# A third kind of unit in the seven-product pairs: one k-tile pair split in halves, in two gate pairs and both projection pairs, and nine instead of eleven matmuls on a constant ahead of the first product

## The chip, the cores and the metric

The kernel runs on one core of a Trainium2 chip. TensorE (PE) multiplies into PSUM; VectorE (DVE), ScalarE (ACT) and GpSimd (POOL) work elementwise; SyncE (SP) issues most loads from HBM on its queue, and POOL's queue issues a few that accumulate. The metric is the device time of one execution in microseconds, the median of several. Before the change it is 1359.29 us (three runs, 1358.73 to 1360.31).

## What is computed

One encoder block over 256 tokens of width 2048, in float32:

```python
h = rms_norm(x, g_mix[layer])
proj = h @ w_in[layer]            # heads of mixers A, B, C, and three gates
...                               # dilated, grouped-query and memory attention: oa, ob, oc
gates = sigmoid(gt).reshape(b, s, N_BRANCH, D_MODEL)
merged = (gates[:, :, 0] * (oa @ w_br_a[layer]) + gates[:, :, 1] * (ob @ w_br_b[layer])
          + gates[:, :, 2] * (oc @ w_br_c[layer]))
x = x + merged @ w_o[layer]
hf = rms_norm(x, g_ffn[layer]) @ w_ffn_in[layer]
x = x + (silu(hf[..., :D_FF]) * hf[..., D_FF:]) @ w_ffn_out[layer]
```

The change touches the gates and the branch products (the merging pairs), the projection by `w_o`, and the first microseconds of the kernel.

## The kernel before

**Products.** A float32 product is three products of rounded operands: ACT writes `whi`, the weight rounded (L433), DVE writes `wlo`, the rest (`raw - whi`, L443), and PE multiplies hi by hi, hi by lo and lo by hi into one PSUM bank (L79). Activations are split once, into two tiles per k-tile pair. A weight block is 128 x 1024: two k-tiles of 512 columns, one load of 512 KB by SP into one of eleven buffers (seven `raw`, two `more`, two halves of `both`); there are five pairs of `whi` and `wlo`. A buffer is free for the next load when its last reader has run, mostly the `wlo` subtraction.

**Pairs.** `pair` computes two blocks of 512 columns (0 and 1) for two halves of the tokens, four PSUM banks. The 2048 rows of weights are eight units of two k-tiles. A *whole* unit of column block 0 or 1 (steps `d0` to `d7` and `D0` to `D7`) takes 12 matmuls of 512 columns. A *double* takes two units and both column blocks together, in seven products X, W, P, Y, Z, Q, H of 6 matmuls for each of its two k-tiles instead of eight (the Winograd form of Strassen's scheme): 42 matmuls per unit pair and column pair and 48 without. It needs sums of tokens (`forms`, made by `token_sums`, and again split into hi and lo) and sums of weights: the first by an accumulating load on POOL's queue, those of P (L576), Q (L578) and H (L580) on DVE, each a 128 x 1024 addition. When the last X, P and Q products of a pair are done, ACT and DVE move partial sums between the banks (L553 to L562).

**Order.** A list of steps stands for each pair: front, back and end. `l0`, `r0` load the four blocks of a double, a letter with a number is a product, and a dot in the front is a place where a step of the end of the pair before it is put. `run` goes through the steps of all pairs of a chain and calls each step's first part (loads, sums, hi on ACT, and lo on DVE one step later) four steps ahead of its matmuls. PE and SP keep this order; on ACT and DVE the splits keep theirs among themselves, and a scheduler sets the rest (evacuations, `sg`, `mg`, transposes) between them.

**Stages.** In the profiled run: keys and values of the memory tokens to 47 us, queries, keys, values and attention to 286, the gates and the product of the first branch for column blocks 0 and 1 to about 313, then five merging pairs (gates of two column blocks in `pair`, with the branch products as dots' fillers and sigmoids and merges at L883 to L903): pair 0 at 313 to 352, pair 1 to 402, pair 2 to 454, pair 3 to 511, pair 4 to 570. Pairs 1 and 2 are those of the second branch; each pair takes the units 0 to 3 as two doubles and 4 to 7 whole. Then two projection pairs by `w_o` (to 614 and 658; one double, six whole units; the residual is added at L947) with the transposes of the result into `x1T` beside them, and the FFN to the end.

**The start.** Eleven matmuls of a 128 x 128 constant, float32 and so two passes each, run into an unused bank (L345 and L346) until the first weights are there. The first unit of column block 0 is loaded and split by k-tile (2 x 128 x 512), that of block 1 whole.

Of the kernel before, what the change touches and what calls it, by code (L numbers as in the profile page):

```python
# [57 lines left out]
STEPS_O = ("l0 X0 . r0 W0 . P0 Y0 . Q0 .", "Z0 D2 H0 D3 d2 D6 d3 D7 D4 D5", "d6 d7 d4 d5")  # L58
STEPS_O2 = ("l0 X0 . r0 W0 . P0 Y0 . Q0 .", "Z0 D2 H0 D3 d2 D4 D5 d3 D6 D7", "d4 d5 d6 d7")
# [44 lines left out]
def encoder_block(ctx: ExitStack, tc: tile.TileContext, a: dict, out: bass.AP):  # L104
# [106 lines left out]

    def release(raw):

        free.append(place_of.pop(id(raw))[1])
# [83 lines left out]
    def transposed(src, dst, g=None, lag=1, also=None):  # L298
# [3 lines left out]
        for h in range(2):  # L302
            if h:
                yield lag
            tp = bank("tp", "tp")
            for k in range(2):
                for t in range(T):
                    nc.tensor.transpose(tp[:, k * S + t * P:k * S + (t + 1) * P],
                                        src[t][:, (2 * h + k) * P:(2 * h + k + 1) * P], ident)
            if g is None:  # L310
                d = dst(2 * h, 2)
                split(d[0], d[1], tp.rearrange("p (k s) -> p k s", s=S))
            else:
                for k in range(2):
                    d = dst(2 * h + k, 1)
                    split(d[0], d[1], tp[:, k * S:(k + 1) * S], g(2 * h + k))
            if also is not None:
                if full is None:
                    full = s4([P, 2, 4, P], "ffull")
                to, of = full[:, :, 2 * h:2 * h + 2], tp.rearrange("p (k t s) -> p k t s", t=T, s=P)  # L320
                if g is None:
                    nc.scalar.activation(to, of, AF.Copy)
                else:
                    for k in range(2):
                        nc.scalar.activation(to[:, k], of[:, k], AF.Copy, scale=g(2 * h + k))
        if also is not None:
            token_sums(full, also)

    def token_sums(full, to):


        raw = s4([P, 2, 4, P], "fraw")
# [12 lines left out]
    for _ in range(11):  # L345
# [74 lines left out]
    def halves(*srcs, each=None):  # L420
# [5 lines left out]
        n = 0  # L426
        for v in srcs:
            v = v.unsqueeze(1) if len(v.shape) == 2 else v
            o = slice(n, n + v.shape[1])
            if each:  # L430
                low(0)
                each(n)
            nc.follow(nc.scalar.activation(hi[:, o], v, AF.Copy))  # L433
            due.append((lo[:, o], v, hi[:, o].bitcast(F32)))
# [5 lines left out]
    def low(n):  # L440

        while len(due) > n:
            nc.follow(nc.vector.tensor_sub(*due.pop(0)))  # L443

    def pair(src, lhs, lists, done, doubles=(), forms=None, operand=None, fresh="", early=False, by_halves=False):
# [12 lines left out]
        left = {"Y": 2 * nd + 2 * wholes["d"], "X": 6 * nd, "V": 2 * nd + 2 * wholes["d"],  # L458
                "W": 4 * nd + 2 * wholes["D"], "Q": 2 * wholes["D"]}
# [3 lines left out]
        stops = {"X": [left["X"] - n * nd for n in (2, 4, 6)], "W": [left["W"] - 2 * nd]}  # L463
# [30 lines left out]
        def whole(u, c):  # L494
            def ready():
# [11 lines left out]
                hi, lo = halves(*(raw[:, k] for k in range(PK)) if parts == 2 else (raw,),  # L507
# [24 lines left out]
        def begin2(m):  # L532
            j = doubles[m][1]
            raws[m].update({"b22": load((src(j, 1),), 0, PK), "b21": load((src(j, 0),), 0, PK)})
# [6 lines left out]
        def phase_end(kind, hi):  # L541
            seen[kind] = seen.get(kind, 0) + 1
            if seen[kind] < nd:
# [19 lines left out]

        def seventh(kind, m):
            of = {"X": "b11", "W": "t", "Y": "b21", "P": "t", "Z": "b22", "Q": "b11", "H": "b21"}[kind]
            bk = {"P": "X", "Q": "X", "H": ends[0][1], "Z": "W"}.get(kind, kind)
            needs = {"Y": "X", "P": "X", "Z": "P", "Q": "P", "H": "Q"}

            def ready():
                r = raws[m]  # L570
                raw = r[of]
# [7 lines left out]
                elif kind == "H":  # L579
                    nc.follow(nc.vector.tensor_add(raw, r["t"], raw))  # L580
                hi, lo = halves(raw)
                for n in {"Q": ["b11"], "Z": ["b22"], "H": ["t", "b21"]}.get(kind, ()):
                    release(r.pop(n))

                def products():
                    assert kind not in needs or seen.get(needs[kind], 0) == nd, (kind, seen)
                    assert kind != "Z" or seen["W"] == nd
                    for i in range(2):
# [4 lines left out]
                        mul(bk, st, hi[:, i], lo[:, i])  # L593
# [5 lines left out]
        def step(o):  # L599
# [5 lines left out]
            if kind in "lr":  # L605
                return lambda: (begin if kind == "l" else begin2)(n)
# [262 lines left out]
    mT, x1T, x, room = {}, [], [], []  # L869
    ss1 = const.tile([P, T, 4], F32, name="ss1")  # L870
    by_room = lambda tiles: lambda m, i, f: (tiles()[m][:, i, 0, (f + 1) % 4], tiles()[m][:, i, 1, (f + 1) % 4])
    TWO = (0, 1), (2, 3)

    def merging():
        nth = 0
        for b, (g0, k0, k1) in enumerate(((0, 0, 2), (8, 2, 6), (4, 6, 12))):
            for j in (0, 2) if b else (2,):
# [16 lines left out]
                def merge(c, r, j, b, sg):  # L894
# [4 lines left out]
                    def later():  # L899
# [4 lines left out]
                        if b == 2:  # L904
                            to = mT[j + c] = s8([P, 2, 4, S], "mT", pool=home(j + c))
                            if j + c == 0:
                                room.extend(form_room(1))
                            yield 4
                            yield from transposed([mg[t][:, n0:n0 + NC] for t in range(T)],
                                                  lambda k, n: (to[:, 0, k:k + n], to[:, 1, k:k + n]),  # L910
                                                  lag=2, also=room[0] if j + c == 0 else None)
                    if b:
                        start(urgent(later()))

                front, back, end = pair(block_pair(a["w_gate"], g0 + j), xT, STEPS_GATE[min(nth, 2)], gates, TWO,
                                        by_room(lambda: gforms), early=nth == 0, fresh="Y" if nth < 2 else "")
# [9 lines left out]
    def projecting():  # L926
# [16 lines left out]
        for n in (0, 2):  # L943
# [22 lines left out]
            yield pair(block_pair(a["w_o"], n), mTl, STEPS_O2 if n else STEPS_O, add, TWO[:1], by_room(lambda: room))  # L966
# [139 lines left out]
```

## Time and profile before

| | |
|---|---|
| median of three runs | 1359.29 us |
| the profiled execution, its own time | 1359.78 us |
| its span, first to last instruction | 1358.0 us |
| PE | 6176 matmul passes |
| DVE, ACT instructions | 1412, 1112 |
| loads | 297.17 MB read from HBM, 221 GB/s over the span |
| slowest stage of DMA shown below | mean share 0.77 of the 16 engines, pair 1 |

| stage | us | DVE busy | ACT busy |
|---|---|---|---|
| pair 0 (313 to 352) | 39.0 | 34.86 | 22.95 |
| pair 1 (352 to 402) | 50.0 | 41.66 | 31.43 |
| pair 2 (402 to 453.6) | 51.6 | 43.25 | 31.27 |
| pair 3 (453.6 to 510.7) | 57.1 | 45.76 | 33.39 |
| pair 4 (510.7 to 569.8) | 59.1 | 51.84 | 37.13 |
| projection 1 (569.8 to 613.8) | 44.0 | 34.19 | 24.23 |
| projection 2 (613.8 to 658) | 44.2 | 36.62 | 30.75 |

How to read the lines of a timeline: start in us, length in us, engine, line of the kernel, operation, output and inputs by their names in the program (buffer numbers left out), shape, count of like instructions in a row; in brackets the idle time of that engine before it and what ended it. A matmul's length is modelled and overlaps the next one's; its pace is read from starts. The page's slices are tenths of busy time of a fortieth of the span.

### The profile page before, as it was taken

To read this page: it belongs to the slowest core of one execution; us is meant where nothing else is said; L and a number is where in the kernel's file an instruction comes from. 1 tells how busy PE (TensorE), PEld (TensorE's weight loads), DVE (VectorE), ACT (ScalarE), POOL (GpSimd) and SP (SyncE) were. 2 spreads that over 40 slices of the span, in tenths; PEclk is the share of its full clock that TensorE was granted. 3 is DMA by queue.
4 is the path that set the end of the run, shared out by engine and by line. 5 is a ranking of instruction groups with operands and counts; after the bars stand their busy time and mean duration, and the time that the engine had idled before them with its cause. 6 is when DMAs were issued, how large, how long until landed. Compare 5 with 4: busy or idle time off the path is not lost.

```text
span 1358.0 us, 17334 instructions
## 1 busy us (share of the span) xinstructions
PE 1351.8 (100%) x6176; PEld 1121.4 (83%) x6176; DVE 1157.1 (85%) x1412; ACT 856.4 (63%) x1112; POOL 53.1 (4%) x60
## 2 busy tenths in 40 slices
PE   9999999999999999999999999999999999999998
PEld 8888888888888888888888888888888888888887
DVE  6878877778879869778899998988999889989997
ACT  7877656656656656657676666555666655566664
POOL 0010000000000000000000000000000000000000
PEclk9999999999999999999999999999999999999999
DMA  9976445556787584785577766688666787666872
GB/s 365 348 231 208 153 146 174 165 171 215 231 264 219 188 293 167 249 279 175 167 232 263 210 208 215 220 263 262 192 218 212 248 263 205 215 230 209 277 221 101
DMA packets 86342, 301.18 MB, mean 222 GB/s; under 512 B 9776, under 2 KB 12336, under 8 KB 86000
## 3 DMA queue, kind: packets, MB, share of 16 engines
q1 hardware_dynamic: 79488, 275.94, 58.1%
q0 software_dynamic: 6624, 24.12, 9.4%
q8 instruction: 48, 0.79, 0.2%
q14 instruction: 38, 0.31, 0.1%
q10 hardware_dynamic: 144, 0.02, 0.0%
HBM read 297.17 MB, written 2.88 MB: 221 GB/s over the span
## 4 chain that ended last, share of the span: by engine, by line
PE 94%; DVE 3%; DMA 1%; issue 1%; ACT 1%; SPq 0%; DVEq 0%; ACTq 0%
PE mmX L79 28%; PE mmW L79 20%; PE mm L79 16%; PE mmY L79 15%; PE mmQ L79 11%; DVE wlo L443 2%; PE tp L79 1%; PE sc L79 1%; PE o L79 1%; DMA raw<-in_w_br 1%; ACT whi L433 1%; PE pT L79 1%; PE hT L79 0%; DMA raw<-in_w_mem 0%; DVE raw L578 0%
## 5 line engine op out<-in xcount | busy, mean ns | idle before, releaser
L433 ACT ACTIVATE whi<-raw 128x1024 fp32r<-128x1024 f32 (+1 forms) x363 | 376.8, 1054 | 235.4 <-PE mmQ L79 53.7
L443 DVE TENSOR_TENSOR wlo<-raw,whi 128x1024 fp32r<-128x1024 f32 (+1 forms) x363 | 437.8, 1220 | 87.9 <-ACT whi L433 82.5
L79 PE MATMUL mm<-whi,xT 128*128 128x512 f32 x640 | 202.3, 393 | 0.0
L433 ACT ACTIVATE whi<-both 128x1024 fp32r<-128x1024 f32 x101 | 106.5, 1055 | 59.0 <-DVE both L578 18.1
L79 PEld LDWEIGHTS mm<-whi,xT 128*128 128x128 f32 x640 | 119.2, 188 | 23.5 <-issue 0.4
L133 DVE TENSOR_TENSOR wlo<-raw,whi 128x1024 fp32r<-128x1024 f32 x82 | 103.3, 1262 | 36.8 <-ACT whi L132 34.3
L443 DVE TENSOR_TENSOR wlo<-both,whi 128x1024 fp32r<-128x1024 f32 x101 | 123.2, 1222 | 11.6 <-ACT whi L433 10.8
L443 DVE TENSOR_TENSOR wlo<-more,whi 128x1024 fp32r<-128x1024 f32 x89 | 108.7, 1222 | 20.9 <-ACT whi L433 19.5
L433 ACT ACTIVATE whi<-more 128x1024 fp32r<-128x1024 f32 x89 | 93.9, 1058 | 50.5 <-PE mmQ L79 15.8
L79 PE MATMUL mm<-wlo,xT 128*128 128x512 f32 x320 | 125.6, 393 | 0.0
L132 ACT ACTIVATE whi<-raw 128x1024 fp32r<-128x1024 f32 x82 | 86.8, 1062 | 56.4 <-PE mm L79 40.3
L79 PE MATMUL mmW<-whi,forms 128*128 128x512 f32 x368 | 122.1, 391 | 0.0
L79 PE MATMUL mmX<-whi,forms 128*128 128x512 f32 x368 | 122.1, 390 | 0.0
L79 PE MATMUL mmX<-whi,x1T 128*128 128x512 f32 x352 | 120.9, 389 | 0.0
L79 PE MATMUL mmY<-whi,x1T 128*128 128x512 f32 x264 | 89.1, 389 | 0.0
L79 PEld LDWEIGHTS mmW<-whi,forms 128*128 128x128 f32 x368 | 69.1, 188 | 14.3
L79 PEld LDWEIGHTS mmX<-whi,forms 128*128 128x128 f32 x368 | 69.1, 188 | 14.3
L79 PEld LDWEIGHTS mmX<-whi,x1T 128*128 128x128 f32 x352 | 66.1, 188 | 13.7
L79 PE MATMUL mmX<-wlo,forms 128*128 128x512 f32 x184 | 71.6, 389 | 0.0
L79 PE MATMUL mmW<-wlo,forms 128*128 128x512 f32 x184 | 71.6, 389 | 0.0
L79 PEld LDWEIGHTS mm<-wlo,xT 128*128 128x128 f32 x320 | 60.2, 188 | 12.4 <-issue 0.7
L79 PE MATMUL mmX<-wlo,x1T 128*128 128x512 f32 x176 | 68.5, 389 | 0.0
(277 smaller groups left out, 2595.2 us busy)
## 6 DMA issues: line engine op xcount, KB each, us to landing
raw<-in_w_ffn SPq DMA_DIRECT2D x116, 512.0 KB, 6.0
raw<-in_w_gate SPq DMA_DIRECT2D x66, 512.0 KB, 4.8
raw<-in_w_qkv SPq DMA_DIRECT2D x64, 512.0 KB, 4.4
raw<-in_w_ffn_out SPq DMA_DIRECT2D x54, 512.0 KB, 6.6
both<-in_w_ffn SPq DMA_DIRECT2D x33, 512.0 KB, 6.4
more<-in_w_ffn SPq DMA_DIRECT2D x27, 512.0 KB, 6.3
raw<-in_w_o SPq DMA_DIRECT2D x22, 512.0 KB, 4.7
both<-in_w_ffn_out SPq DMA_DIRECT2D x20, 512.0 KB, 5.5
```

Of the source, the lines that this page charges most:

```text
L79: ins = op(*args, **kw)
L132: nc.scalar.activation(hi, src, AF.Copy)
L133: nc.vector.tensor_sub(lo, src, hi.bitcast(F32))
L433: nc.follow(nc.scalar.activation(hi[:, o], v, AF.Copy))
L443: nc.follow(nc.vector.tensor_sub(*due.pop(0)))
```

## The change

Four things change.

1. **Singles.** In merging pairs 1 and 2 the unit 4 (k-tiles 8 and 9) and in both projection pairs the unit 2 are no longer whole: its two k-tiles are taken as the two halves of one product scheme, seven products of 3 matmuls, 21 for the 24 of `D` and `d`. Steps: `s0` loads both blocks (`t`, column block 1, and `b1`, column block 0), `S1` does X and W, `S2` P and Y, `S3` Q and Z, `S4` H. Each part makes one half-wide sum on DVE (128 x 512) and splits one or two half-wide operands. A new list of steps, `STEPS_GATE5`, serves pairs 1 and 2; pairs 3 and 4 keep the list they had.
2. **Token sums for them.** `lone_of_gates` makes those of the gates on DVE beside pair 0 (`glone`: an addition 128 x 512, one 128 x 256, two 128 x 128, and a split into hi and lo); those of `w_o` (`lone`) come with a transpose of `mT` beside pair 4.
3. **Buffers.** Four more load buffers (`gate0` to `gate3`) during pairs 0 to 2, given up ahead of pair 3.
4. **The front.** Nine matmuls on the constant instead of eleven, and the first unit of column block 1 is split by k-tile as well; the lo parts of one operand now leave the waiting list together.

The diff, cut to its core (the steps named `a` stand in no list):

```diff
@@ -53,10 +53,10 @@
-    ("l0 l1 X0 . . X1 r0 W0 r1 W1 P0 P1 . Y0 Q0 Q1 Y1", "Z0 Z1 D4 H0 D5 H1 D6 D7", "d4 d5 d6 d7"),
     ("l0 l1 X0 X1 . r0 W0 r1 W1 P0 P1 . Y0 Y1 . Q0 Q1 .", "Z0 Z1 D4 H0 D5 H1 D6 D7", "d4 d5 d6 d7")]
-STEPS_O = ("l0 X0 . r0 W0 . P0 Y0 . Q0 .", "Z0 D2 H0 D3 d2 D6 d3 D7 D4 D5", "d6 d7 d4 d5")
-STEPS_O2 = ("l0 X0 . r0 W0 . P0 Y0 . Q0 .", "Z0 D2 H0 D3 d2 D4 D5 d3 D6 D7", "d4 d5 d6 d7")
+STEPS_GATE5 = ("l0 l1 s0 X0 . X1 S1 r0 W0 r1 W1 . P0 P1 S2 . Y0 Y1 Q0 Q1 S3", "Z0 Z1 D5 H0 D6 H1 D7 S4", "d5 d6 d7")
+STEPS_O = ("l0 s0 X0 S1 . r0 W0 . P0 S2 Y0 . Q0 S3 .", "Z0 D3 H0 D6 S4 d3 D7 d6 D4 D5", "d7 d4 d5")
+STEPS_O2 = ("l0 s0 X0 S1 r0 W0 . P0 S2 Y0 . Q0 S3 .", "Z0 D3 H0 D4 S4 d3 D5 D6 D7", "d4 d5 d6 d7")
...
-    for _ in range(11):
+    for _ in range(9):
         nc.tensor.matmul(idle[:, :P], lhsT=ident, rhs=ident, start=True, stop=True)
...
-                hi, lo = halves(*(raw[:, k] for k in range(PK)) if parts == 2 else (raw,),
+                hi, lo = halves(*(raw[:, k] for k in range(PK)) if operand and u == 0 else (raw,),
...
+        def begin_single(_):
+            t = load((src(single[0], 1),), 0, PK)
+            raws["s"] = {"t": t, "b1": load((src(single[0], 0),), 0, PK)}
...
+        def part(n):
+            kinds = ("XW", "PY", "QZ", "H")[n - 1]
+            def ready():
...
+                if n == 1:
+                    nc.follow(nc.vector.tensor_add(t[:, 0], t[:, 0], b1[:, 0]))
+                elif n == 2:
+                    nc.follow(nc.vector.tensor_add(t[:, 0], t[:, 0], t[:, 1]))
+                elif n == 3:
+                    nc.follow(nc.vector.tensor_sub(b1[:, 0], t[:, 0], b1[:, 0]))
+                elif n == 4:
+                    nc.follow(nc.vector.tensor_add(b1[:, 1], t[:, 0], b1[:, 1]))
+                hi, lo = halves(*((b1[:, 0], t[:, 0]), (t[:, 0], b1[:, 1]), (b1[:, 0], t[:, 1]), (b1[:, 1],))[n - 1])
...
+    def lone_of_gates():
+        yield 6
+        to = lone["gate"] = s8([P, 1, 2, 4, P], "glone", pool=tail)
+        one, tl = s4([P, 1, 4, P], "ffull"), xT.tiles[2].bitcast(F32)
+        nc.vector.tensor_add(one[:, 0].rearrange("p (k t) s -> p k (t s)", t=T), tl[:, :2, 0], tl[:, :2, 1])
+        yield 2
+        token_sums(one, to)
...
+        start(lone_of_gates())
+        parts = [s8([P, 2, PK, NC], "both", F32, tail) for _ in range(2)]
+        extra = [(Part(r[:, i]), f"gate{2 * n + i}") for n, r in enumerate(parts) for i in range(2)]
+        free.extend(extra)
...
+                if nth == 3:
+                    retired.extend(extra)
+                    free[:] = [f for f in free if f not in extra]
```

Where the order of instructions moves, DVE is shown at three places. Each row is a line of the kernel (its number, before or after the change), the operation, output and inputs with their buffer's number, and the shape.

At the start of the program, before the change (`raw1` is the first unit of column block 1):

```order
L443 TENSOR_TENSOR wlo_126<-raw0_122,whi_125 128x512 x2
L443 TENSOR_TENSOR wlo_139<-raw1_134,whi_138 128x1024
L136 SCALAR_TENSOR_TENSOR memT_112<-rawT_136,gT_82,memT_112 128x256 x2
L443 TENSOR_TENSOR wlo_149<-raw2_142,whi_148 128x1024
L443 TENSOR_TENSOR wlo_157<-raw3_152,whi_156 128x1024
```

and with it:

```order
L455 TENSOR_TENSOR wlo_124<-raw0_120,whi_123 128x512 x2
L455 TENSOR_TENSOR wlo_137<-raw1_132,whi_136 128x512 x2
L136 SCALAR_TENSOR_TENSOR memT_110<-rawT_134,gT_82,memT_110 128x256 x2
L455 TENSOR_TENSOR wlo_148<-raw2_141,whi_147 128x1024
L455 TENSOR_TENSOR wlo_157<-raw3_152,whi_156 128x1024
```

The lo of the block in `raw1` is two instructions of 512 columns in place of one of 1024.

In merging pair 0, before the change, from the lo of P0 (out of `raw0`) to those of Q0 (`raw1`), Q1 (`raw3`) and Z0 (`raw4`):

```order
L443 TENSOR_TENSOR wlo_3374<-raw0_3326,whi_3373 128x1024
L443 TENSOR_TENSOR wlo_3388<-raw2_3331,whi_3387 128x1024
L443 TENSOR_TENSOR wlo_3400<-both_3324,whi_3399 128x1024
L443 TENSOR_TENSOR wlo_3412<-raw5_3345,whi_3411 128x1024
L578 TENSOR_TENSOR raw1_3328<-raw0_3326,raw1_3328 128x1024
L443 TENSOR_TENSOR wlo_3429<-more0_3353,whi_3428 128x1024
L558 TENSOR_TENSOR mmW_3391<-m5_3409,mmX_3365 128x512
L578 TENSOR_TENSOR raw3_3333<-raw2_3331,raw3_3333 128x1024
L443 TENSOR_TENSOR wlo_3440<-raw1_3328,whi_3439 128x1024
L443 TENSOR_TENSOR wlo_3452<-raw3_3333,whi_3451 128x1024
L443 TENSOR_TENSOR wlo_3468<-raw4_3343,whi_3467 128x1024
```

and with it, from the lo of d4's block in `both` on:

```order
L455 TENSOR_TENSOR wlo_3402<-both_3324,whi_3401 128x1024
L343 TENSOR_TENSOR fraw_3472<-fraw_3472,ffull_3441 128x128
L455 TENSOR_TENSOR wlo_3414<-raw5_3347,whi_3413 128x1024
L647 TENSOR_TENSOR raw1_3330<-raw0_3328,raw1_3330 128x1024
L455 TENSOR_TENSOR wlo_3431<-more0_3355,whi_3430 128x1024
L344 TENSOR_TENSOR fraw_3472<-fraw_3472,ffull_3441 128x128
L619 TENSOR_TENSOR mmW_3393<-m5_3411,mmX_3367 128x512
L647 TENSOR_TENSOR raw3_3335<-raw2_3333,raw3_3335 128x1024
L455 TENSOR_TENSOR wlo_3445<-raw1_3330,whi_3444 128x1024
L133 TENSOR_TENSOR glone_3440<-fraw_3472,glone_3440 128x512
L455 TENSOR_TENSOR wlo_3457<-raw3_3335,whi_3456 128x1024
L455 TENSOR_TENSOR wlo_3479<-raw4_3345,whi_3478 128x1024
```

Between the lo of P0 and Q0 four instructions of the token sums have come in (the addition into `ffull` and the 128 x 256 one stand just ahead of the rows shown), and the lo of `glone` between Q0's and Q1's.

In merging pair 2, before the change, from a whole unit's lo in `both` to Z0's (`raw3`):

```order
L443 TENSOR_TENSOR wlo_4124<-both_3324,whi_4123 128x1024
L558 TENSOR_TENSOR mmW_4104<-m5_4121,mmX_4061 128x512
L578 TENSOR_TENSOR raw2_3966<-raw4_3964,raw2_3966 128x1024
L443 TENSOR_TENSOR wlo_4136<-raw0_4133,whi_4135 128x1024
L578 TENSOR_TENSOR both_3324<-raw5_3969,both_3324 128x1024
L443 TENSOR_TENSOR wlo_4148<-raw2_3966,whi_4147 128x1024
L443 TENSOR_TENSOR wlo_4165<-both_3324,whi_4164 128x1024
L443 TENSOR_TENSOR wlo_4177<-raw1_4174,whi_4176 128x1024
L443 TENSOR_TENSOR wlo_4187<-raw3_4030,whi_4186 128x1024
```

and with it, from the last whole unit ahead of Q0 to Z0's (`both_3326`); `wlo_4252` belongs to S3, `sg` and `mg` are the merge of the branch:

```order
L455 TENSOR_TENSOR wlo_4205<-raw6_4106,whi_4204 128x1024
L619 TENSOR_TENSOR mmW_4146<-m5_4173,mmX_4097 128x512
L647 TENSOR_TENSOR more1_4005<-both_3327,more1_4005 128x1024
L455 TENSOR_TENSOR wlo_4216<-raw5_4001,whi_4215 128x1024
L580 TENSOR_TENSOR both_3327<-raw0_4008,both_3327 128x512
L981 TENSOR_TENSOR sg_4243<-br_4047,sg_4243 128x512 x2
L455 TENSOR_TENSOR wlo_4228<-more1_4005,whi_4227 128x1024
L987 TENSOR_TENSOR mg0_2851<-mg0_2851,sg_4243 128x512
L455 TENSOR_TENSOR wlo_4252<-both_3327,whi_4251 128x512
L987 TENSOR_TENSOR mg1_2852<-mg1_2852,sg_4243 128x512
L455 TENSOR_TENSOR wlo_4252<-raw0_4008,whi_4251 128x512
L455 TENSOR_TENSOR wlo_4263<-both_3326,whi_4262 128x1024
```

Three half-wide instructions of S3 (its sum at L580 and two lo parts) and the four merge operations of the branch, which before came after Z0, stand ahead of Z0's lo.

106 lines of the change are left out of this document (80 added, 26 removed).

## The prediction

> **What bounds the kernel now.** I read the page first (busy shares, the chain), then the waits of PE, then the timeline around each of them, and last, for every place where DVE works without a pause, how long before its first use each operand is finished.
>
> ```profile
> PE 1351.8 (100%) x6176; PEld 1121.4 (83%) x6176; DVE 1157.1 (85%) x1412; ACT 856.4 (63%) x1112; POOL 53.1 (4%) x60
> PEclk9999999999999999999999999999999999999999
> PE 94%; DVE 3%; DMA 1%; issue 1%; ACT 1%; SPq 0%; DVEq 0%; ACTq 0%
> PE mmW L79 <- DVE wlo L443: 0.8, 2, 0.4
> 402.05 2.72 PE mmX L79 x12
> ```
>
> The first three lines are of the page, the fourth is from the waits of PE over the whole run (in us, times, longest), the last a link of the chain. TensorE is the bound: 94% of the chain, its clock never throttled in the record, and behind the start only two waits, of 0.4 us each, on DVE. Twelve matmuls of 512 columns take 2.72 us, **0.2267 us each**. So a matmul left out is worth 0.2267 us, if DVE and ACT go on delivering in time. DVE is busy for 85% of the span, so that condition is the question. Below, the *lead* of an operand is the time from the end of its lo subtraction on DVE to the first matmul that reads it.
>
> **Matmuls.** Four single units (two gate pairs, two projection pairs) of 21 matmuls stand in for D and d of 12 each: 4 x 3 = 12 fewer, 12 x 0.2267 = **-2.72 us**.
>
> **The front.**
>
> ```profile
> 1.36 5.07 PE L79 MATMUL idle<-ident 128*128 128x128 f32 x22 [1.36 <-POOL ident masks.py:199]
> 4.55 1.14 ACT L433 ACTIVATE whi<-raw 128x512 fp32r<-128x512 f32 x2
> 6.08 1.09 PE L79 MATMUL mmY<-whi,memT 128*128 128x512 f32 x2
> 7.01 0.40 PE L79 MATMUL mmY<-wlo,memT 128*128 128x512 f32 x1
> 7.68 1.06 ACT L433 ACTIVATE whi<-raw 128x1024 fp32r<-128x1024 f32 x1 [1.99 <-DMA raw<-in_w_mem]
> 8.77 1.23 DVE L443 TENSOR_TENSOR wlo<-raw,whi 128x1024 fp32r<-128x1024 f32 x1 [2.28 <-ACT whi L433]
> 9.28 0.39 PE L79 MATMUL mmW<-whi,memT 128*128 128x512 f32 x1
> 10.05 0.50 PE L79 MATMUL mmW<-wlo,memT 128*128 128x512 f32 x1 [0.38 <-DVE wlo L443]
> 10.71 2.52 DVE L443 TENSOR_TENSOR wlo<-raw,whi 128x1024 fp32r<-128x1024 f32 x2
> 12.94 0.39 PE L79 MATMUL mmY<-wlo,memT 128*128 128x512 f32 x1
> ```
>
> Eleven idle matmuls are 22 passes between 1.36 and 6.08, 0.215 us a pass; two fewer let the first product start 4 x 0.215 = 0.86 us earlier, at 5.22. Its operands allow that: the first hi half is ready at about 5.1 (half of ACT's 1.14 from 4.55). But the first two products took 6.08 to 7.01, 0.46 us each, twice the later pace. If that slow pace ends by the clock, 0.86 us bring two matmuls forward and not four: 0.43 us. If it ends with the work done, the whole 0.86. The row of granted clocks reads 9 (90% or more) in the first slice too and doesn't tell the two apart.
>
> [...]
>
> Which case holds decides little, because of the next wait. Column 1's first block is landed at 7.68; now it is split by k-tile: first hi half to 8.27 (1.14 for two), first lo half 0.69 later (the 512-wide row below), 8.96 to 9.0, against 10.00 now. mmW's first hi·lo product then starts at about 9.05 whichever case holds (by PE itself at 9.28 + 0.23 - 0.43 = 9.08), against 10.05, and the restart loses another 0.11 there in 10.05 to 10.39. Gain up to there 1.0 to 1.1. What is late next: the second unit's lo (10.71, ends 11.93, used 12.94), which then is wanted at 11.9, while ACT's extra instruction moves it some 0.07 later, to 12.0. I take **-0.9 us** (bounds -0.45 to -1.1).
>
> **The stall at D4 of pair 1.**
>
> ```profile
> 376.74 0.39 PE L79 MATMUL mmW<-whi,xT 128*128 128x512 f32 x1
> 377.50 0.50 PE L79 MATMUL mmW<-wlo,xT 128*128 128x512 f32 x1 [0.38 <-DVE wlo L443]
> 377.84 0.63 PE L79 MATMUL mmW<-whi,xT 128*128 128x512 f32 x2
> ```
>
> 0.76 + 0.34 us where two matmuls take 0.45: 0.65 us lost. D4 is gone and four more load buffers serve pairs 0 to 2, so the loads that ACT waited for ahead of this pair are issued sooner: **-0.65 us**; what the new steps cost there comes below.
>
> **What DVE takes on.** Per single: four half-wide sums and seven half-wide lo subtractions for two whole lo ones; and the token sums of the gates, in pair 0.
>
> ```profile
> 34.19 0.29 DVE L370 TENSOR_TENSOR turns<-rope,gh 128x128 f32<-128x128 f32 x1
> 34.39 0.29 DVE L371 SCALAR_TENSOR_TENSOR turns<-rope,gh 128x128 f32<-128x128 f32 x1
> ...
> 328.55 4.79 DVE L443 TENSOR_TENSOR wlo<-raw,whi 128x1024 fp32r<-128x1024 f32 x4
> 334.99 0.69 DVE L562 TENSOR_TENSOR mmQ<-m,mmX 128x512 f32<-128x512 f32 x1
> 335.58 1.22 DVE L580 TENSOR_TENSOR raw<-raw,raw 128x1024 f32<-128x1024 f32 x1
> 336.72 1.22 DVE L443 TENSOR_TENSOR wlo<-more,whi 128x1024 fp32r<-128x1024 f32 x1
> ...
> 330.50 0.39 PE L79 MATMUL mmX<-wlo,forms 128*128 128x512 f32 x1
> 338.66 0.39 PE L79 MATMUL mmW<-wlo,xT 128*128 128x512 f32 x1
> ```
>
> Back to back, starts are 0.60 us apart at 512 wide (334.99, 335.58), 1.14 at 1024 (335.58, 336.72), 0.20 at 128; 256 wide lies between, I take 0.35. So a single costs DVE 11 x 0.60 - 2 x 1.14 = 4.3 us, while PE gains 0.68: wherever DVE has no slack, a single loses more than it saves.
>
> [...]
>
> *Pair 0* (token sums of the gates). Q0's lo ends at 328.55 + 1.22 = 329.77 and is used at 330.50: lead 0.73; D4's ends at 337.94, used at 338.66: 0.72. DVE has no pause between. The order puts 0.60 + 0.35 + 0.20 + 0.20 = 1.35 us ahead of Q0's lo and another 0.60 behind it, so 1.95 by D4: 1.95 - 0.72 = **+1.2 us** of waiting (0 if the queue reaches P0 earlier than now, 1.7 at full durations).
>
> *Pair 2.*
>
> ```profile
> 404.54 1.22 DVE L443 TENSOR_TENSOR wlo<-raw,whi 128x1024 fp32r<-128x1024 f32 x1
> 408.92 0.39 PE L79 MATMUL mmW<-wlo,forms 128*128 128x512 f32 x1
> ...
> 430.80 1.22 DVE L443 TENSOR_TENSOR wlo<-raw,whi 128x1024 fp32r<-128x1024 f32 x1
> 433.40 0.39 PE L79 MATMUL mmW<-wlo,xT 128*128 128x512 f32 x1
> ```
>
> W1's lo now has a lead of 408.92 - 405.76 = 3.16, and D5's, the smallest, 433.40 - 432.02 = 1.38. In the new order, from W1's lo to Z0's stand 13 whole and 11 half operations on DVE: 13 x 1.14 + 11 x 0.60 = 21.4 us; PE has 78 matmuls, 17.7 us, in the same stretch. 3.16 + 17.7 - 21.4 = -0.55. Z1 wins back 0.2, D5 (H0's sum and a lo, 2.27, against 1.36) loses 0.9. Together **+1.2 us** (0 to 2.2). *Pair 1* by the same sum from a lead of some 3.4 at W1 (the wait for loads gone) ends at 0: +0.1 and, with the 0.8 that ACT's load waits may still take, I put **+0.3** (0 to 0.9). Pairs 3 and 4 keep smallest leads of 0.3 and 0.6 by the sum: nothing.
>
> *Projections and the first FFN pair.*
>
> ```profile
> 569.80:613.80 44.00, 44.00 (x203) 36.42 (x202) 34.19 (x37) 24.23 (x27) 0.86 (x1) 1.00 0.73 251
> ```
>
> That is the window of the first projection pair (length, then busy time of PE, PE's weight loads, DVE, ACT, POOL); the rows below are of the second and of the first FFN pair.
>
> ```profile
> 622.31 0.48 DVE L136 SCALAR_TENSOR_TENSOR x1T<-tp,gT,x1T 128x256 fp32r<-128x256 f32 x1 [0.54 <-ACT x1T L135]
> 623.62 0.48 DVE L136 SCALAR_TENSOR_TENSOR x1T<-tp,gT,x1T 128x256 fp32r<-128x256 f32 x1 [0.83 <-ACT x1T L135]
> 625.79 1.23 DVE L443 TENSOR_TENSOR wlo<-raw,whi 128x1024 fp32r<-128x1024 f32 x1 [1.68 <-ACT whi L433]
> ...
> 690.12 1.22 DVE L443 TENSOR_TENSOR wlo<-raw,whi 128x1024 fp32r<-128x1024 f32 x1
> 691.40 0.50 PE L79 MATMUL mmW<-wlo,x1T 128*128 128x512 f32 x1
> ```
>
> In the first projection pair DVE is busy for 34.19 us of 44.00; the single's 4.3 us stay under it: nothing. In the second, the transposes of x1 make DVE wait 0.54 + 0.83 + 1.68 = 3.05 us; with a lead of about 3 when they come, as W1 of pair 2 has it, nothing is left: **+0.4** (0 to 1.5). In the FFN's first pair a lo ends 0.06 us before its use (691.34, 691.40): any shift in DVE's order there shows, **+0.3** (0 to 0.6).
>
> **The sum.** -2.72 - 0.9 - 0.65 + 1.2 + 1.2 + 0.3 + 0.4 + 0.3 = -0.87 us. The profiled execution took 1359.78 us (the span of the table ahead and 1.8 around it), so 1358.9; it lay 0.49 above the median of 1359.29, which gives **1358.4 us** on the median's footing.
>
> **Rivals.** *The cover holds* (chance 0.27): the four more buffers let ACT and DVE enter each front with leads at the buffers' limit, so that pair 0 and pair 2 never run dry. For it: W1 of pair 2 has a lead of 3.16 even now, and the tail steps that fill the front give DVE 1.6 us each. Against: pair 0's DVE is without a pause well before Q0. Gains of 4.27 less some 0.5 us left at the FFN: 1355.5. *The half-wide steps don't run back to back* (0.07, the slower side): each part is a sum on DVE, a hi on ACT and a lo on DVE in turn, and where nothing stands between them DVE waits as in the 622.31 row, 0.54 us each. Three parts ahead of the smallest lead in pairs 1 and 2 and in the second projection are 9 x 0.54 = 4.9 us on top, 1363; it is slower by over 0.2% from 3.6 us, seven handovers, on. Against: the order puts another operation between most of them. *The front gives nothing* (0.10): if the idle passes leave PE slow for longer, its 0.9 go: 1359.3. The forecast keeps 0.56.
>
> 0.2%, about what a measurement of this kernel can tell from no change, is 2.7 us: faster is below 1356.6, slower above 1362.0. The first rival and a small part of the forecast's own spread give faster 0.27; same 0.66; slower 0.07. The range, 1355.2 to 1361.0, reaches from the first rival to the forecast with the upper bounds of pairs 1, 2 and the second projection.
>
> **What would show it.** Right: mmW's first lo product at about 9.1; PE waits for DVE's lo near Q1 and D4 of pair 0 and near Z0 and D5 of pair 2, one us or so each; none at D4 of pair 1; 16 fewer PE passes. Wrong: no waits there (the first rival), or DVE idle between a half-wide sum and its lo (the second).

## The result and the profile after

The changed kernel takes **1366.38 us** (median of six runs, 1366.18 to 1367.89) against 1359.30 for the kernel before on the same chip (six runs, 1358.73 to 1360.34): 1.0053 times as long, interval 1.0040 to 1.0066. It is 7.1 us slower; the forecast was 0.9 us faster, and the range ended at 1361.0. Its profiled execution took 1366.36 us with a span of 1364.6, 6.6 us more than the span before.

Two lines of the page, then the longest waits of PE over the whole run but the one at its start (us in total, times, longest):

```profile
PE 1352.7 (99%) x6160; PEld 1118.5 (82%) x6160; DVE 1177.2 (86%) x1458; ACT 864.6 (63%) x1136; POOL 53.1 (4%) x60
PE 95%; DVE 3%; issue 1%; ACT 1%; POOL 0%; DVEq 0%; ACTq 0%; POOLq 0%
```

```profile
PE mmW L79 <- DVE mT L133: 1.2, 1, 1.2
PE mmW L79 <- ACT mT L132: 1.2, 1, 1.2
PE mmY L79 <- DVE wlo L455: 1.2, 1, 1.2
PE mmQ L79 <- DVE mg L981: 1.2, 1, 1.2
PE mmW L79 <- DVE wlo L455: 0.6, 2, 0.4
PE tp L79 <- DVE mg L987: 0.5, 1, 0.5
```

The 16 passes fewer are there (6160 for 6176: twelve matmuls and two idle matmuls of two passes), and the share of PE in the chain barely moves. What the page hides, the waits show: where two waits of 0.4 us stood there are now four of 1.2 and some small ones. All but the fifth line name things that no term of the prediction holds: the transposed merge (`mT`), a Y product in pair 4, which has no single, and the merge itself (`mg`, twice).

All of PE's start-to-start distances in the trace, less what the same matmuls take without a wait, give this account (us; a restart after a wait costs 0.11 more, as from 329.58 to 329.92 where 0.23 is the pace, and is in it):

| place | predicted | trace |
|---|---|---|
| twelve matmuls fewer | -2.72 | -2.72 |
| front | -0.9 | -1.33 |
| pair 0 | +1.2 | +1.0 |
| pair 1, old stall at D4 | -0.65 | -0.65 |
| pair 1, new | +0.3 | +1.44 |
| pair 2 | +1.2 | +1.19 |
| pairs 3 and 4 | 0 | +0.11, **+2.58** |
| projection 1 | 0 | **+4.64** |
| projection 2, first FFN pair | +0.4, +0.3 | 0, +0.15 |
| sum | -0.87 | +6.4 of the 6.6 found |

It compares one execution with one; what of it differs between executions is said below.

**The front, pair 0 and pair 2 came about as worked out.** The timeline at the start of the program (start, length, engine, line, output and inputs; in brackets the idle time ahead and what ended it):

```profile
5.37 0.83 PE L79 MATMUL mmY<-whi,memT 128*128 128x512 f32 x2
7.21 1.15 ACT L444 ACTIVATE whi<-raw 128x512 fp32r<-128x512 f32 x2 [0.69 <-DMA raw<-in_w_mem]
8.72 0.40 PE L79 MATMUL mmW<-wlo,memT 128*128 128x512 f32 x1
11.52 0.50 PE L79 MATMUL mmY<-wlo,memT 128*128 128x512 f32 x1
```

The block of column 1 is rounded from 7.21 on, where it had landed at 7.68 before, so its lo is no longer late: mmW's first lo product starts at 8.72, where it was 10.05, and the second unit's, at 11.52 for 12.94, is hardly held up. The early landing is luck in part: with the same front the second unit's product starts at 11.72 in e5's trace, and in e6's the rounding of that block begins at 8.42 and the product starts at 12.74. PE in pair 0 and pair 2:

```profile
329.58 0.50 PE L79 MATMUL mmX<-wlo,forms 128*128 128x512 f32 x1 [0.26 <-DVE wlo L455]
```

```profile
430.92 0.50 PE L79 MATMUL mmW<-wlo,forms 128*128 128x512 f32 x1 [0.17 <-DVE wlo L455]
434.32 0.50 PE L79 MATMUL mmW<-wlo,xT 128*128 128x512 f32 x1 [0.39 <-DVE wlo L455]
```

These are Q0 (a second, smaller wait at Q1), Z0 and D5, each after a lo at the end of an unbroken row on DVE.

**Pair 1 waits for a bank.** PE there before, then PE and DVE after:

```profile
356.11 0.39 PE L79 MATMUL mmW<-whi,oT 128*128 128x512 f32 x1
...
360.42 0.39 PE L79 MATMUL mmW<-whi,forms 128*128 128x512 f32 x1
```

```profile
358.05 0.39 PE L79 MATMUL mmW<-whi,glone 128*128 128x512 f32 x1
...
361.66 1.82 DVE L455 TENSOR_TENSOR wlo<-raw,whi 128x1024 fp32r<-128x1024 f32 x2
363.40 0.68 DVE L981 TENSOR_TENSOR mg<-mmW,sg 128x512 f32<-128x512 f32 x1
364.14 0.50 PE L79 MATMUL mmQ<-whi,oT 128*128 128x512 f32 x1 [1.17 <-DVE mg L981]
```

The W and Q banks of a pair and of the branch products (`oT`) come out of the same two PSUM buffers (in the kernel, `bank` gives both one tag with two buffers). S1 reads `glone` and opens the pair's W bank at 358.05; before, the first whole unit of the branch (356.11) came ahead of the pair's first W (360.42). Now the pair's W holds one buffer and the branch's W the other. So the branch's Q product stands on PE until DVE has merged the branch's W (363.40 + 0.68), and DVE has two lo subtractions ahead of that merge.

**Pair 4 waits for the token sums of the projection.** DVE in pair 4, and the PE row that waits:

```profile
522.54 0.69 DVE L133 TENSOR_TENSOR mT<-tp,mT 128x512 fp32r<-128x512 f32 x1 [0.38 <-ACT mT L132]
...
524.91 0.69 DVE L133 TENSOR_TENSOR lone<-fraw,lone 128x512 fp32r<-128x512 f32 x1 [0.70 <-ACT lone L132]
526.35 1.22 DVE L455 TENSOR_TENSOR wlo<-raw,whi 128x1024 fp32r<-128x1024 f32 x1 [0.74 <-ACT whi L444]
```

```profile
530.50 0.50 PE L79 MATMUL mmY<-wlo,xT 128*128 128x512 f32 x1 [1.22 <-DVE wlo L455]
546.16 0.55 PE L79 MATMUL tp<-ident,mg 128*128 128x128 f32 x3 [0.52 <-DVE mg L987]
```

`token_sums` for the singles of `w_o` runs inside `transposed`. Its three additions and its lo are about 1.7 us of work, but DVE also stands 0.38, 0.70 and 0.74 us for ACT, which rounds `mT`, `lone` and the next weights in turn. The lo of a Y product is then 1.2 us late, and what DVE does late brings the next merge late too (546.16).

**Projection 1 waits for a chain through three engines.** PE before, then PE, ACT and DVE after (`tp<-ident,mg` are the four transposes that become the last `mT` blocks; the next mmW opens a whole unit):

```profile
607.92 0.60 PE L79 MATMUL tp<-ident,mg 128*128 128x128 f32 x4
608.27 0.48 PE L79 MATMUL mmW<-whi,mT 128*128 128x512 f32 x1
...
611.12 0.39 PE L79 MATMUL mmW<-whi,mT 128*128 128x512 f32 x1
```

```profile
615.86 0.60 PE L79 MATMUL tp<-ident,mg 128*128 128x128 f32 x4
617.70 0.50 PE L79 MATMUL mmW<-whi,mT 128*128 128x512 f32 x1 [1.24 <-ACT mT L132]
...
619.68 0.53 PE L79 MATMUL mmW<-whi,mT 128*128 128x512 f32 x1 [1.25 <-DVE mT L133]
```

```profile
616.11 1.06 ACT L444 ACTIVATE whi<-raw 128x1024 fp32r<-128x1024 f32 x1 [1.66 <-PE mmQ L79]
617.07 0.58 ACT L132 ACTIVATE mT<-tp 128x512 fp32r<-128x512 f32 x1
```

```profile
617.19 1.23 DVE L455 TENSOR_TENSOR wlo<-raw,whi 128x1024 fp32r<-128x1024 f32 x1 [0.24 <-ACT whi L444]
618.34 0.69 DVE L578 TENSOR_TENSOR raw<-raw 128x512 f32<-128x512 f32 x1
618.94 0.68 DVE L133 TENSOR_TENSOR mT<-tp,mT 128x512 fp32r<-128x512 f32 x1
```

The unit that reads those blocks is D5. Before, D4 stood between the transposes and D5, 608.27 to 611.12; now D5 comes right behind them. So PE stands for ACT's rounding (behind a weight block on ACT), starts, and stands again for DVE's rest (behind a weight block and a sum of 512 columns on DVE).

D5 is the tenth step behind d7, the end of the last gate block, in both lists. The second group of transposes came behind the eighth before (Z0 D2 H0 D3 d2 D6 d3 D7) and comes behind the ninth now (Z0 D3 H0 D6 S4 d3 D7 d6 D4). The job that issues it asks for the same number of steps as before. But `tick` lets one waiting job go on per step, and the three steps of `rows`, the loads of the residual `x`, come first. Followed through the program's list of waiting jobs, they held this one up by two steps before and hold it up by three now, since the two counts meet at another step. The one step more takes the whole unit out from between. Behind the two waits PE's granted clock is 0.50 for 3.41 us, 1.6 us of the 4.64; the last section shows it.

### The profile page after: what moved, and what is told of

Same layout as the page of the kernel before. It is cut to its first block, busy times and chain, and to the rows that moved or that the text cites. A ratio compares the mean times of both kernels' runs of the same rounds, so it can differ in the third digit from the quotient of the medians.

```text
span 1364.6 us, 17362 instructions
## 1 busy us (share of the span) xinstructions
PE 1352.7 (99%) x6160; PEld 1118.5 (82%) x6160; DVE 1177.2 (86%) x1458; ACT 864.6 (63%) x1136; POOL 53.1 (4%) x60
## 4 chain that ended last, share of the span: by engine, by line
PE 95%; DVE 3%; issue 1%; ACT 1%; POOL 0%; DVEq 0%; ACTq 0%; POOLq 0%
PE mmX L79 28%; PE mmW L79 20%; PE mm L79 16%; PE mmY L79 15%; PE mmQ L79 11%; DVE wlo L455 2%; PE tp L79 1%; PE sc L79 1%; PE o L79 1%; ACT whi L444 1%; PE pT L79 1%; PE hT L79 0%; PE mmV L79 0%; PE idle L79 0%; DVE raw L647 0%
## 5 line engine op out<-in xcount | busy, mean ns | idle before, releaser
L444 ACT ACTIVATE whi<-raw 128x1024 fp32r<-128x1024 f32 (+1 forms) x352 | 357.1, 1032 | 210.7 <-PE mmQ L79 47.3
L455 DVE TENSOR_TENSOR wlo<-raw,whi 128x1024 fp32r<-128x1024 f32 (+1 forms) x352 | 414.2, 1191 | 73.5 <-ACT whi L444 70.6
L444 ACT ACTIVATE whi<-both 128x1024 fp32r<-128x1024 f32 (+1 forms) x118 | 120.3, 1026 | 66.2 <-DVE both L647 14.8
L455 DVE TENSOR_TENSOR wlo<-both,whi 128x1024 fp32r<-128x1024 f32 (+1 forms) x118 | 139.1, 1184 | 16.2 <-ACT whi L444 15.1
L444 ACT ACTIVATE whi<-more 128x1024 fp32r<-128x1024 f32 (+1 forms) x104 | 107.4, 1038 | 60.9 <-DVE more L649 18.8
L455 DVE TENSOR_TENSOR wlo<-more,whi 128x1024 fp32r<-128x1024 f32 (+1 forms) x104 | 124.7, 1200 | 14.8 <-ACT whi L444 13.7
```

Source lines behind the costliest of these rows:

```text
L455: nc.follow(nc.vector.tensor_sub(*part))
```

## The experiments

**Theory A**: each loss has a place in the order (transposes, bank, token sums), and moving that one thing gives the time back. **Theory B**: DVE has no room for the singles, and a wait that is moved appears elsewhere. All times are medians; the kernel before had 1359.18, 1359.13 and 1359.36 in the three groups of runs.

**e1_d5**: one more unit between the transposes and D5.

```diff
-STEPS_O = (..., "Z0 D3 H0 D6 S4 d3 D7 d6 D4 D5", "d7 d4 d5")
+STEPS_O = (..., "Z0 D3 H0 D6 S4 d3 D7 d6 D4 d7 D5", "d4 d5")
```

> The changed kernel with one step moved: in the first projection pair D5, which reads the second half of the last transposed block right behind its transposes, changes places with d7. Theory A (order: PE stands behind two handovers to ACT and DVE with nothing to multiply, and its clock falls to 0.54 for the 3.5 us behind them): the 3.0 us of waiting and the 1.6 us of slow matmuls go, about 1361.8 us. Theory B (DVE is overloaded, and any order only moves the wait): PE waits as long a few steps on, 1365 or more.

1365.45 us (1365.03 to 1365.53), ratio 1.0046 [1.0031, 1.0061]. PE's waits:

```profile
PE mmY L79 <- DVE wlo L455: 1.9, 2, 1.2
PE mmW L79 <- DVE wlo L455: 1.8, 4, 1.0
...
```

Both `mT` waits are gone, but PE loses 3.65 us in projection 2 that it did not lose before. d7 is no longer there to fill that pair's front; that its DVE runs late for this reason is argued, and fits e5, which leaves d7 in place and loses 0.97 there. That is B's answer, for this edit.

**e5_tp**: the same chain, mended without taking a step from the next pair: these transposes one step earlier.

```diff
-                            yield 4
+                            yield 3 if j + c == 2 else 4
```

> The changed kernel with the transposes of the last merged block (column block 2) one step earlier, which brings them back to where they stood before the change, two whole units ahead of D5; no list of steps is changed. Theory A (the loss in the first projection pair is the place of these transposes): its 4.6 us go and nothing comes in their place, about 1361.8 us. Theory B (the second projection pair lacks DVE time for its single, and the pause ahead of it was what it lived on): some 3.5 us of waits for lo come back there, as when D5 was moved, about 1365.3 us.

1362.80 (1362.40 to 1363.65), ratio 1.0026 [1.0017, 1.0035], 3.6 under the changed kernel:

```profile
PE mmY L79 <- DVE wlo L455: 1.9, 2, 1.2
...
PE mmQ L79 <- DVE mg L981: 1.2, 1, 1.2
...
```

The `mT` waits, which stood at the head of this view, are gone: D4 stands between the transposes (613.33) and D5 (616.52) again. Of the 4.64 us only a new 0.97 in projection 2 (an mmY product) is given back. A holds for the larger part; the place of the transposes is the cause of the largest loss.

**e2_bank**: pair 1 with its two early dots ahead of S1, so that the branch opens its banks first.

```diff
+STEPS_GATE5A = ("l0 l1 s0 X0 . . X1 S1 r0 W0 r1 W1 P0 P1 S2 . Y0 Y1 Q0 Q1 S3",) + STEPS_GATE5[1:]
-                                        STEPS_GATE5 if nth in (1, 2) else STEPS_GATE[min(nth, 1)], gates, TWO,
+                                        STEPS_GATE5A if nth == 1 else STEPS_GATE5 if nth == 2 else STEPS_GATE[min(nth, 1)], gates, TWO,
```

> The changed kernel with the first branch unit D0 of pair 1 put ahead of S1, which opens the pair's W bank. Theory A (two PSUM banks serve W and Q of the pair and of the branch; with the pair's W open first, the branch's Q has to wait until its W is merged): the wait of 1.33 us at mmQ goes, with its restart of 0.11, about 1364.9 us, and no wait on the merge is left in pair 1. Theory B (the merge is late because DVE is): PE waits for it or for a lo elsewhere in pair 1, 1366 us.

1366.10 (1365.70 to 1368.10), ratio 1.0050 [1.0033, 1.0067]. The line `mmQ <- mg` is gone from the waits, so the bank order is its cause; but 0.75 us of waits for `wlo` come in later in pair 1, and the gain of 0.3 is within the spread. The profiled execution is the slowest of the four and has two waits for the residual `x`, 0.7 us in all, that the changed kernel's trace does not have. Half A, half B.

**e3_lone**: the projection's token sums eight steps after the transposes instead of among them.

```diff
-                token_sums(one, single)
+        if single is not None:
+            yield 8
+            token_sums(one, single)
```

> The changed kernel with the token sums of w_o (four operations and a split, made inside the transposes of mT beside pair 4) eight steps later. Theory A (they stand in DVE's order between a transpose and the lo that PE waits for, each waiting for ACT in turn): 1.8 us at mmY in pair 4 go, and most of the 0.7 at the transposes behind it, about 1364.2 us. Theory B (the amount of DVE work in pair 4 is too much wherever it stands): the wait moves back by some steps, 1366 us.

1363.43 (1362.30 to 1365.75), ratio 1.0031 [1.0020, 1.0043]: 2.95 under the changed kernel. Neither wait of pair 4 is in its profile and none replaces them: A. They are 2.58 of the 2.95; the slower clock of projection 1 is missing in this trace too (1.00 from 613 to 621 us), and can be the rest.

**e4_all**: e1, e2 and e3 together.

> All three moves together. Theory A: the gains add, 4.6 + 1.4 + 2.2 = 8.2 us, about 1358.2 us, about 1 us faster than before the change. Theory B: under half of that, 1363 or more.

1362.28 (1361.56 to 1364.47), ratio 1.0023 [1.0014, 1.0033]: 4.1 above what A expected; the waits of e1 in projection 2 stay.

**e7_nogate** and **e8_noproj**: the changed kernel without the singles of the gates (old lists for pairs 1 and 2, no token sums in pair 0, the four buffers kept), and without those of the projections and their token sums.

```diff
...
-        start(lone_of_gates())
...
-                                        STEPS_GATE5 if nth in (1, 2) else STEPS_GATE[min(nth, 1)], gates, TWO,
+                                        STEPS_GATE[min(nth, 2)], gates, TWO,
```

> The changed kernel without the two gate singles and their token sums (old lists for pairs 1 and 2), with the four more load buffers. By the stalls of the profile the gate singles cost 0.9 (token sums) + 1.4 (bank) + 1.2 (DVE) - 1.4 (six matmuls) = 2.1 us: 1364.3 us, if the buffers by themselves take away the old wait of 0.65 at D4 of pair 1; 1364.9 if they don't and it was D4's going that did.

```diff
-STEPS_O = ("l0 s0 X0 S1 . r0 W0 . P0 S2 Y0 . Q0 S3 .", "Z0 D3 H0 D6 S4 d3 D7 d6 D4 D5", "d7 d4 d5")
-STEPS_O2 = ("l0 s0 X0 S1 r0 W0 . P0 S2 Y0 . Q0 S3 .", "Z0 D3 H0 D4 S4 d3 D5 D6 D7", "d4 d5 d6 d7")
+STEPS_O = ("l0 X0 . r0 W0 . P0 Y0 . Q0 .", "Z0 D2 H0 D3 d2 D6 d3 D7 D4 D5", "d6 d7 d4 d5")
+STEPS_O2 = ("l0 X0 . r0 W0 . P0 Y0 . Q0 .", "Z0 D2 H0 D3 d2 D4 D5 d3 D6 D7", "d4 d5 d6 d7")
...
-                                                  single=lone["w_o"] if j + c == 1 else None)
+                                                  single=None)
```

> The changed kernel without the two projection singles and their token sums (old lists for both projection pairs). By the stalls of the profile they cost 2.6 (pair 4) + 4.6 (first projection pair) - 1.4 (six matmuls) = 5.8 us: 1360.6 us. If the second projection pair too paid in the changed kernel, less remains, down to 1360.

1364.28 (1362.69 to 1364.67) and 1360.88 (1360.05 to 1361.46), ratios 1.0035 [1.0021, 1.0048] and 1.0012 [1.0003, 1.0022]. So, with their token sums, the gate singles cost 2.1 us and the projection singles 5.5, where each two should have saved 1.36 in matmuls. The two sum to 7.6, which with k9's 1.0 below accounts for the 7.1 of the whole change to within 0.5.

**e6_front**: the kernel before with the new front alone (the lo parts leave the waiting list together, as in the change).

```diff
-    for _ in range(11):
+    for _ in range(9):
...
-                hi, lo = halves(*(raw[:, k] for k in range(PK)) if parts == 2 else (raw,),
+                hi, lo = halves(*(raw[:, k] for k in range(PK)) if operand and u == 0 else (raw,),
```

> The kernel before with the front alone: nine matmuls on the constant and block 1's first unit split by k-tile. Both theories: the 1.3 us that the profile of the changed kernel shows at the start, 1358.0 us; if the profile caught a lucky start, 1358.9.

1358.98 (1357.92 to 1360.87), ratio 0.9998 [0.9988, 1.0007]. The profiled execution was the slowest of the ten. ACT and PE at its start, PE in pair 1, and ACT ahead of pair 1:

```profile
8.42 1.15 ACT L435 ACTIVATE whi<-raw 128x512 fp32r<-128x512 f32 x2 [2.50 <-DMA raw<-in_w_mem]
12.74 0.50 PE L79 MATMUL mmY<-wlo,memT 128*128 128x512 f32 x1
```

```profile
378.73 0.50 PE L79 MATMUL mmW<-wlo,xT 128*128 128x512 f32 x1 [0.77 <-DVE wlo L446]
```

```profile
349.86 1.06 ACT L435 ACTIVATE whi<-raw 128x1024 fp32r<-128x1024 f32 x1 [5.56 <-DMA raw<-in_w_gate]
```

In this execution the block of column 1 was rounded from 8.42 on, and the second unit's product came only 0.2 us earlier than before (12.74 for 12.94): most of the microsecond was never won. Pair 1 then lost 1.9 us, where it had lost 0.65: the wait at D4 grew from 0.38 to 0.77, and ACT stood 5.56 us for the load of the gate's weights, 2.28 before. So the median fits the second expectation, that the changed kernel's profile caught an early start. Whether the faster executions win the microsecond at the front and lose it in pair 1 no trace shows.

**k9_base**: the new front and the four buffers, no single anywhere (the edits of e7 and e8 together).

> The front and the four more load buffers without any single: the changed kernel with the old lists everywhere. In the front alone PE reached pair 1 earlier and waited 1.9 us there on lo's and a bank's partial sum, against 0.65 before the change, so that the front's 1.3 us came back as waiting. Theory A (pair 1 starts late for want of loads, and the buffers let them start sooner): the wait shrinks to 0.4 as in the run without gate singles, 1357.7 us. Theory B (DVE sets pair 1's pace whatever the loads do): about 1359, as the front alone.

1358.33 (1358.14 to 1358.79), ratio 0.9992 [0.9983, 1.0002]. What is left of the old stall:

```profile
376.20 0.50 PE L80 MATMUL mmW<-wlo,xT 128*128 128x512 f32 x1 [0.17 <-DVE wlo L456]
```

No load holds ACT up ahead of pair 1 any more. Of the 0.65 us of the old stall 0.44 stay with their restart, so most of that term was D4's going and not the buffers. The time is 1.0 below the kernel before, with an interval that still touches 1. Against e6, which differs in the buffers alone, the median is 0.65 lower and the spread 0.65 us and not 2.95: this fits buffers that let the front's gain through, but the two intervals overlap, and it isn't shown.

**k10_proj**: k9 with both projection singles, e3's place of the token sums and e5's of the transposes. **k12_proj1**: the same with the old list in projection 2.

```diff
-STEPS_O2 = ("l0 s0 X0 S1 r0 W0 . P0 S2 Y0 . Q0 S3 .", "Z0 D3 H0 D4 S4 d3 D5 D6 D7", "d4 d5 d6 d7")
+STEPS_O2 = ("l0 X0 . r0 W0 . P0 Y0 . Q0 .", "Z0 D2 H0 D3 d2 D4 D5 d3 D6 D7", "d4 d5 d6 d7")
```

> That with both projection singles, the token sums of w_o eight steps later and the last block's transposes one step earlier. Theory A (each loss of the projection singles had its place): six matmuls less, -1.4, and the 1.0 us of waiting that the run with earlier transposes showed in the second projection pair, so 0.4 below the run without singles, 1357.3 us if that is 1357.7. Theory B (DVE's load): 1 to 2 us above it.

> As the run with both projection singles, but the second projection pair keeps its old list. If the 1.0 us of waiting there belongs to its own single, it goes together with the three matmuls saved, 0.3 us below the run with both; if it comes from the shorter first pair, it stays, and the time is 0.7 above.

1358.40 (1357.98 to 1359.02), ratio 0.9993 [0.9984, 1.0002]; and 1359.70 (1359.14 to 1360.50), ratio 1.0002 [0.9993, 1.0012]. Two singles save 1.36 us of matmuls, and k10 is no faster than k9. DVE and PE in projection 2 of k10, then the wait of k12:

```profile
622.76 0.88 DVE L137 SCALAR_TENSOR_TENSOR x1T<-tp,gT,x1T 128x256 fp32r<-128x256 f32 x2 [0.62 <-ACT x1T L136]
625.98 1.23 DVE L458 TENSOR_TENSOR wlo<-raw,whi 128x1024 fp32r<-128x1024 f32 x1 [1.71 <-ACT whi L447]
```

```profile
627.26 0.50 PE L80 MATMUL mmY<-wlo,mT 128*128 128x512 f32 x1 [0.70 <-DVE wlo L458]
```

```profile
PE tp L80 <- DVE x L1041: 1.3, 1, 1.3
```

The handovers of x1 (ACT rounds, DVE subtracts, in turn) cost DVE 0.62 and 1.71 us there, and PE waits 0.70 for the next lo. Without the second single that wait is gone, but PE waits 1.3 us for the residual sum `x` that DVE does late, so k12 fits neither of its cases. Why k12 has this wait and k10 not stays open; e2's trace has waits of the same kind.

**k11_full**: the changed kernel with e2, e3, e5 and pair 0's token sums seven steps sooner (6 and 2 steps to 1 and 1), ahead of W0, where DVE has idle time.

```diff
     def lone_of_gates():
-        yield 6
+        yield 1
...
-        yield 2
+        yield 1
         token_sums(one, to)
```

> The changed kernel with all four singles and every wait that was found moved: D0 ahead of S1 in pair 1, transposes one step earlier, token sums of w_o later, and those of the gates some steps earlier, in DVE's idle time ahead of W0 of pair 0. Theory A: 1366.4 - 4.6 + 1.0 - 2.5 - 0.7 - 0.9 = 1358.7 us, no wait at Q0 and Q1 of pair 0, and those at Z0 and D5 of pair 2 left. Theory B: 1361 or more, with waits at other lo's of pairs 0 to 2.

1358.84 (1358.24 to 1360.30), ratio 0.9996 [0.9986, 1.0005]: four edits of the order take 7.5 us away, as much as the change had lost. PE's waits:

```profile
PE mmW L80 <- DVE wlo L458: 1.3, 4, 0.5
PE mmY L80 <- DVE wlo L458: 0.7, 1, 0.7
PE mmX L80 <- DVE wlo L458: 0.2, 1, 0.2
```

Two of the mmW waits lie elsewhere in this execution, 0.15 us at the start of the program and 0.54 at 1340 us. The others come with the restarts to 2.8 us (0.76 in pair 1, 1.1 in pair 2, 0.97 in projection 2). They all name DVE's lo, and they are as large as the 2.72 of matmuls that the four singles save. A for what the change lost, and B fits what it could have won: k9, k10 and k11, with no, two and four singles, lie within 0.5 us. That no other order could win it isn't shown.

## Why the prediction was wrong, point by point

**Matmuls, front, old stall**: right in kind. The front gave 1.33 in the trace and not 0.9: the block of column 1 was there 0.47 us sooner than the term took it to be. That size is luck in part, since ACT could round that block from 7.21 on here and from 8.42 on in e6's execution; the first product came at 5.37 and not at 5.22, because its hi half was ready at 5.31. And the term was booked as if it reached the end by itself: the front alone (e6) was 0.15 us below the kernel before, inside the noise, and with the buffers (k9) 1.0.

**Pair 0 and pair 2**: near in place and right in size, 1.0 for 1.2 (at Q0 and Q1, with 0.07 left at D4) and 1.19 for 1.2 (at Z0 and D5). Both sums, leads less the DVE operations put in between at their start-to-start distances (0.60 and 1.14 us), are thereby borne out. With the full duration of each instruction instead (0.69, 0.42, 0.28, 0.28 and 0.69 us in the changed kernel's trace), pair 0's wait would by estimate have been 2.36 - 0.72 = 1.64 us, near the 1.7 that the prediction set beside its 1.2; the trace has 1.0.

**Pair 1**: +0.3 predicted, +1.44 found, another mechanism. The sum was made for DVE's stream of lo subtractions only. That S1 writes the pair's W bank ahead of the branch, and that the branch's Q then waits for a merge, can be read from the two lists (the second dot, right behind X0 before, stands behind X1, S1 and both W now), and was not looked for. e2 shows the cause; what it brings back is small, since pair 1 then runs into the wait that the sum had been about.

**Pairs 3 and 4: "nothing"** failed at pair 4, by 2.58. The lead sum left out the token sums of `w_o`, which run in `transposed` during pair 4, though those of the gates were counted in pair 0. Counting 1.7 us for them against a lead of 0.6 would have shown a wait of about a microsecond; the three handovers of 0.38, 0.70 and 0.74 us make up the rest. e3 shows the place, not the split between the two.

**Projection 1: "the single's 4.3 us stay under it: nothing"** is the step that failed most, by 4.64. It compared DVE's busy time with the length of the stage, 34.19 of 44.00 us. That average says nothing of the one place where PE waits on a chain from its own transposes through ACT and DVE, and D4 was the cover of that chain. The list that was read for its products still ends in `D4 D5`. What moved is the second group of transposes, by one step against the list, because its job shares the steps with the loads of `x`. e5 shows it: one step back, and both waits are gone. Part of the 4.64, 1.6 us, is the granted clock of 0.50 behind those waits.

**Projection 2 and the first FFN pair**: 0 and 0.15 us for 0.4 and 0.3, inside their bounds. In projection 2 the pauses of projection 1 hid the cost: with those mended it is 0.97 (e5, k10, k11), inside the bounds too.

**Rivals.** The slower rival, handovers between ACT and DVE, was given 0.07 and placed at the parts of the singles, nine of 0.54. Handovers did cost time, but where token sums and transposes are split, in pair 4 and projection 1. The range held only terms of DVE's throughput; no term stood for a producer moved nearer to its reader, on another engine than DVE.

## What to carry to other kernels

When a list of steps gets more or shorter steps, look up everything that counts steps, and what else waits for the same steps, and for each such thing work out in matmuls what lies between its last producer and its first reader, before and after; a stage's busy share can't show that. A new first writer of a bank is a change in the order of banks, so check who now waits for which merge. And where DVE had a lead of a microsecond or so, a product form that trades 0.7 us of matmuls for 4 us of vector work did no better than come out even, in k9 to k11.

## What the runs showed that was not expected

The granted clock fell in the middle of the run. Stretches of the changed kernel in projection 1 (length, busy time of PE, its weight loads, DVE, ACT and POOL with instructions, granted clock, share of DMA, GB/s), then of e7, which has the same two pauses 2.3 us sooner:

```profile
616.60:620.00 3.40, 1.05 (x3) 0.59 (x4) 2.79 (x4) 1.05 (x2) 0.00 (x0) 1.00 0.21 23
620.00:623.42 3.42, 3.42 (x10) 2.66 (x8) 0.69 (x1) 0.72 (x2) 0.00 (x0) 0.50 0.35 131
```

```profile
612.00:615.42 3.42, 2.18 (x12) 1.62 (x10) 2.95 (x3) 1.71 (x3) 0.00 (x0) 1.00 0.00 0
615.42:618.83 3.41, 2.15 (x8) 1.51 (x9) 2.12 (x4) 0.00 (x0) 0.00 (x0) 1.00 0.36 123
```

After two pauses of 1.24 and 1.25 us PE's clock is 0.50 for 3.41 us, in which eight matmuls start, 0.43 us apart, where fifteen would fit at 0.23. In e7 and e3 PE pauses alike, twice for 1.24 or 1.25 us, and the clock stays at 1.00 (e7 from 613 to 623.2 us, e3 from 613 to 621). So the drop did not come behind such pauses in every execution, and e3's runs spread over 3.4 us: the slowest, 1365.75, has a mean granted clock of 0.997, the fastest, 1362.30, one of 1.000. In the 3.40 us ahead of the drop PE was busy for 1.05 us, in the two stretches of e7 around its pauses for 2.18 and 2.15. What brings the drop about, and whether the pauses have a part in it, isn't shown; that it is luck of the execution whether a run pays the 1.6 us is the author's estimate from e3's runs.

In the trace's record of granted clocks the drop lasts 3.413 us, the full clock ahead of it 614.40, from 5.61 to 620.00, and behind it 740.69; in the trace of the kernel before the full clock lasts 1351.68 us, from 6.90 on. That is 180, 217 and 396 times the 3.413 us. Whether it is so in other executions isn't shown.

The half pace at the start ends at different times too. In the traces of the kernel before, of the changed kernel and of e5 PE's first matmul is at 1.36 us. Before, the first two products take 0.93 us (6.08 to 7.01; at the later pace two take 0.46), and the record of granted clocks begins, at full clock, at 6.90; in the changed kernel they take 0.73 (5.37 to 6.10), and it begins at 5.61; in e5, whose front is the same, they take 1.01 (5.29 to 6.30). So in these traces the pace ends neither after a fixed time from the first matmul nor after a fixed amount of work, the question on which the prediction's front term was left open.
